# A hybrid trunk layer on one core: w_out begins with P1 and P2, gates run eight tiles ahead, and the last part keeps its written order

## The chip, the cores and the metric

The kernel runs on one core of a Trainium2 chip. The metric is device time in microseconds for one execution of the whole program; three runs of the kernel before gave 2539.71, 2540.99 and 2543.15 us, so the median is 2540.99 us.

## The reference, cut to what matters

One layer for 512 tokens of width 2048, in float32. Two branches read the same normalised input `h`; the change lies in the second half of branch B and in everything behind it.

```python
proj = h @ w_in                                   # 16 kinds of columns, gates among them
...
y_a = o_a @ w_br_a                                # branch A
u = silu(layernorm(conv(glu))) * silu(z_b)
y_b = u @ w_br_b                                  # branch B
gate_a, gate_b = split(sigmoid(gate_logits + b_gate))
mixed = (gate_a * y_a + gate_b * y_b) @ w_out
x = x + rmsnorm(mixed, g_post)
e = p @ w_ple_proj
x = x + rmsnorm(sigmoid(x @ w_ple_gate) * e, g_ple)
```

## The kernel before, in words

**Matrix products.** Every float32 operand is split into a high part (ACT casts it) and a low part (DVE subtracts the cast from the value), and a product is three matmuls: high by high, high by low, low by high. A weight block of 128x1024 floats (512 KB) is loaded by the SP queue into a buffer `raw` (three of them) and split by ACT and DVE into a pair of pieces. Up to branch B the pieces are called `w` (L125, L126), and a tile of 128 output channels by 512 tokens is 48 matmuls of 128x512 (`gemm_cm`, L178, L180 and L182). PSUM gives these tiles two banks (`gps`, L160).

**Branch B.** For each of 16 tiles there is a gate tile (columns of `w_in`, evacuated by ACT with a sigmoid, L700, into a buffer `gt`) and a tile of `w_br_b`, evacuated by DVE: product with the gate (L824), then sum onto branch A's tile (L826). The sum is the tile of `mixed`. The gate tiles run two ahead of the `w_br_b` tiles.

**w_out.** This product of 2048 by 2048 by 512 is done by a scheme of Strassen and Winograd's kind with seven products: in each half `jp` of the output columns there are P1, Q5, P6, P7, P3, P2 and Q4. The left operands come from quarters of `mixed` and their sums (A11, A12, A22, S1 to S4), formed by `split_a`, `split_b` and `split_c`. The right operands are blocks of `w_out` (B11, B12, B22, B21) or sums of them: a tile `t` (B11 plus B12, L972, to which a DMA of POOL that accumulates adds B22 and later B21), and the sum of B12 and B22 for P7 (`sum_t3`, L981). A product is four pieces, and a piece is 12 matmuls, split by `split_piece` (ACT L1016, DVE L1017) three or four pieces ahead. Of the loads after the first eight, every fourth goes to a buffer `rw`, of which there is one. The first half goes (P1, Q5), (P6, P7, P3), (P2, Q4); the second goes (P1, Q5), (P6, P3), (P2), (P7), (Q4). The products in one bracket take turns, piece by piece.

**What becomes of them.** ACT copies the results of P1 and Q5 out of PSUM (`snap`, L1062). DVE adds and subtracts the others (L1066, L1070). `out_fin` then squares a finished tile on ACT with a running sum (L1085) and multiplies it by the broadcast row of `g_post` (`grow`, loaded by the ACT queue, L930) in place on DVE (L1086). When a token group is complete, its RMS factor is formed (L936, L937, POOL L939), `post` adds the residual (L1113; `xr` is x loaded again), and TensorE transposes the result (`x1t`, L1119). The product with `w_ple_gate` follows (L1196 to L1198), the last quarter of which keeps its weights (`hold`), so that the tail of the last token group is short (`ple_last`, L1234 to L1238).

**What sets the order.** The code is written as one sequence of instructions. A scheduler moves the instructions of each engine against that sequence, going by its own estimate of when each can start; each engine then runs its queue strictly in the order it was given.

Of the kernel before, what the change touches and what calls it, by code (L numbers as in the profile page):

```python
# [15 lines left out]
P = 128  # L16
# [66 lines left out]
def _body(ctx, tc, A, out):  # L83
# [19 lines left out]
    nc.gpsimd.memset(mhalf_c, -0.5)  # L103

# [592 lines left out]
    def evac_gate(dst, i, col):  # L697
# [57 lines left out]
    def layer_norm():  # L755
# [35 lines left out]
        rstd = s2.tile([P, T], F32, tag="s2", name="rstd")  # L791
        nc.scalar.copy(rstd, prs)
        yield
        for i in range(NK):
# [9 lines left out]
            ul = low(LOP if i < 32 - LOP else 0, "ul")  # L804
# [40 lines left out]
    def split_a():  # L845
        for k2 in range(4):
            ah = hpool.tile([P, T], F32R, tag="h", name="ah")
            al = hpool.tile([P, T], F32R, tag="h", name="al")
            s1 = slots.tile([P, T], F32, tag="s", name="sf")
            for n in range(2):  # L850
                kk = 2 * k2 + n
                while not (kk in added and kk + 8 in added):
                    yield
                c = slice(n * 256, n * 256 + 256)
                nc.vector.tensor_tensor(s1[:, c], mixed[kk][:, HI], mixed[kk + 8][:, HI], ALU.subtract)
                nc.scalar.copy(ah[:, c], mixed[kk][:, LO])
                nc.vector.tensor_tensor(al[:, c], mixed[kk][:, LO], ah[:, c].bitcast(F32), ALU.subtract)
                yield
            Sf[k2] = s1
            AW["A11"][k2] = (ah, al)  # L860
            AW["S1"][k2] = sw_split(hpool, "h", s1)
            yield

    def split_b():
        for k2 in range(4):
            s1 = Sf.pop(k2)
            s3_ = s3.tile([P, T], F32, tag="s3", name="sf")
            for n in range(2):
                kk = 2 * k2 + n
                c = slice(n * 256, n * 256 + 256)  # L870
                nc.vector.tensor_tensor(s3_[:, c], mixed[kk][:, LO], mixed[kk][:, HI], ALU.subtract)
                nc.vector.tensor_tensor(s1[:, c], s1[:, c], mixed[kk][:, LO], ALU.subtract)
            AW["S3"][k2] = sw_split(hpool, "h", s3_)
            yield
            AW["S2"][k2] = sw_split(hpool, "h", s1)
            for n in range(2):
                kk = 2 * k2 + n
                c = slice(n * 256, n * 256 + 256)
                nc.vector.tensor_tensor(s1[:, c], mixed[kk + 8][:, LO], s1[:, c], ALU.add)
            AW["S4"][k2] = sw_split(slots, "s", s1)  # L880
            yield

    def split_c():
        for kk in range(8):
            CC[kk] = sw_split(*((slots, "s") if kk < 4 else (s3, "s3")), mixed[kk + 8])
            yield
# [3 lines left out]
    def gate_b_tile(i):  # L890
        gemm_cm(w_in_tile(GATE_TILE0 + 16 + i), hT, evac_gate(gate_b, i, 16 + i))

    gate_b_tile(order[0])
    gate_b_tile(order[1])
# [33 lines left out]
    def bcast_row(src, j, home=S3_):  # L928
        t = unit(home, "grow")
        nc.scalar.dma_start(t, src[:, j * T:(j + 1) * T].broadcast_to([P, T]))  # L930
        return t

    def inv_rms(ss, tag):
        n = ss.shape[1]
        tot = fsm.tile([P, n], F32, name="tot" + tag)
        nc.vector.tensor_reduce(tot, ss, AX, ALU.add)  # L936
        nc.vector.tensor_scalar(tot, tot, 1.0 / D, EPS, ALU.mult, ALU.add)  # L937
        r = fsm.tile([P, n], F32, name="rms" + tag)
        nc.gpsimd.tensor_tensor(r, tot, mhalf_c[:, 0:n], ALU.pow)  # L939
        return r  # L940
# [4 lines left out]
    entries = deque()  # L945
    sources = deque()
# [3 lines left out]

    def load(jp, blk, q):
        loads[0] += 1
        if early[0] or loads[0] % 4:
# [3 lines left out]
        nc.sync.dma_start(raw, WO[jp, blk, q])  # L957
        return raw

    early = [True]  # L960
    loads = [0]

    def acc(t, jp, blk, q):
        nc.gpsimd.dma_start(t, WO[jp, blk, q], accum_op=ALU.add)

    def e_a(jp, q):
        early[0] = jp == 0
        b11 = load(jp, B11, q)
        b12 = load(jp, B12, q)
        early[0] = False  # L970
        t = tb[q] = s3.tile([P, 1024], F32, tag="t", name="t", bufs=4)
        nc.vector.tensor_tensor(t, b11, b12, ALU.add)  # L972
        return [b11, t]

    def e_63(jp, q):
        acc(tb[q], jp, B22, q)
        return [tb[q], load(jp, B22, q)]

    def sum_t3(jp, q, b22):
        b12 = load(jp, B12, q)  # L980
        nc.vector.tensor_tensor(b12, b12, b22, ALU.add)  # L981
        return b12

    def e_b(jp, q):
        acc(tb[q], jp, B22, q)
        b22 = load(jp, B22, q)
        return [tb[q], sum_t3(jp, q, b22), b22]

    def e_p7(jp, q):
        return [sum_t3(jp, q, load(jp, B22, q))]  # L990

    def e_p2(jp, q):
        acc(tb[q], jp, B21, q)
        return [load(jp, B21, q)]

    def e_t(jp, q):
        return [tb[q]]

    def e_c(jp, q):
        return e_p2(jp, q) + [tb[q]]  # L1000

    def split_piece():
# [4 lines left out]
        for m in range(2):  # L1007
            if n < 8:
# [7 lines left out]
        nc.scalar.copy(hi, src)  # L1016
        nc.vector.tensor_tensor(lo, src, hi.bitcast(F32), ALU.subtract)  # L1017
# [42 lines left out]
    def snap(home, ps):  # L1060
        t = unit(home, "snap")
        nc.scalar.copy(t, ps)  # L1062
        return t

    def add(dst, a, b):
        nc.vector.tensor_tensor(dst, a, b, ALU.add)  # L1066
        return dst

    def minus(dst, a, b):
        nc.vector.tensor_tensor(dst, a, b, ALU.subtract)  # L1070
# [10 lines left out]
    def out_fin(jp, gp):  # L1081
        def f(tt, n, c):
            j = 2 * jp + n
            junk = unit(S3_, "fjunk")
            nc.scalar.activation(junk, c, AF.Square, accum_out=ssm[:, tt, j:j + 1])  # L1085
            nc.vector.tensor_tensor(c, c, gp[n], ALU.mult)  # L1086
# [14 lines left out]
    def load_x_again(tts):  # L1101
        xr = {}
        for j in range(4):
            for tt in tts:
                xr[tt, j] = unit(HP_, "xr")
                nc.sync.dma_start(xr[tt, j], rows(A["x"], tt, j))
        return xr

    def post(tts, xr):
        rm = inv_rms(ssm[:, tts[0]:tts[0] + 2, :], f"m{tts[0]}")  # L1110
        for j in range(4):
            for n, tt in enumerate(tts):
                nc.vector.scalar_tensor_tensor(x1[tt][j], x1[tt][j], rm[:, n:n + 1], xr.pop((tt, j)), ALU.mult, ALU.add)  # L1113
            yield
            for k2 in (2 * j, 2 * j + 1):
# [5 lines left out]
                nc.scalar.copy(xh, ps)  # L1121
                xl = unit(HP_, "xl", F32R)
                nc.vector.tensor_tensor(xl, ps, xh.bitcast(F32), ALU.subtract)
# [13 lines left out]
    for e, jp in ((e_a, 0), (e_b, 0), (e_c, 0), (e_a, 1), (e_63, 1), (e_p2, 1), (e_p7, 1), (e_t, 1)):  # L1137
        stage(e, jp)

    gen = split_b()  # L1140
    ps = run(("P1", "Q5"), stepper(gen))
    drain(gen)
    s1 = [snap(S3_, x) for x in ps["P1"]]
    s5 = [snap(S3_, x) for x in ps["Q5"]]
    gp = [bcast_row(A["g_post"], j) for j in (0, 1)]
    fin = out_fin(0, gp)
    gen = split_c()
    ps = run(("P6", "P7", "P3"), stepper(gen))
    drain(gen)
    u2 = [add(unit(S3_, "u2"), ps["P6"][t], s1[t]) for t in range(2)]  # L1150
# [5 lines left out]
    ps = run(("P2", "Q4"))  # L1156
    for t in range(2):
# [185 lines left out]
```

## Time and profile before

| | |
|---|---|
| runs | 2539.71, 2540.99, 2543.15 us |
| the profiled execution | 2539.74 us, of it the span 2537.1 us |
| mean granted TensorE clock | 0.997 |
| TensorE busy | 2495.0 us, 98% of the span, 12202 matmuls and transposes |
| VectorE busy | 1652.4 us, 65% |
| ScalarE busy | 1056.8 us, 42% |
| moved by DMA | 279.45 MB, 110 GB/s on average |

Times in a row of the trace are microseconds from the start of the span. "start, duration, engine, line, operation, out<-in" is the form of a row of the timeline; a bracket at its end says how long the engine had been idle and what ended the wait. Matmuls overlap, so the duration of one (0.39 us) is longer than the step from one start to the next; the steps count.

### The profile page before, as it was taken

To read this page: it belongs to the slowest core of one execution; us is meant where nothing else is said; L and a number is where in the kernel's file an instruction comes from. 1 tells how busy PE (TensorE), PEld (TensorE's weight loads), DVE (VectorE), ACT (ScalarE), POOL (GpSimd) and SP (SyncE) were. 2 spreads that over 40 slices of the span, in tenths; PEclk is the share of its full clock that TensorE was granted. 3 is DMA by queue.
4 is the path that set the end of the run, shared out by engine and by line. 5 is a ranking of instruction groups with operands and counts; after the bars stand their busy time and mean duration, and the time that the engine had idled before them with its cause. 6 is when DMAs were issued, how large, how long until landed. Compare 5 with 4: busy or idle time off the path is not lost.

```text
span 2537.1 us, 32634 instructions
## 1 busy us (share of the span) xinstructions
PE 2495.0 (98%) x12202; PEld 2035.7 (80%) x12202; DVE 1652.4 (65%) x3092; ACT 1056.8 (42%) x2083; POOL 140.6 (6%) x151
## 2 busy tenths in 40 slices
PE   8999999999999999999999999999999999999998
PEld 7878787777878777888888888887888888787887
DVE  6765767666676765977786868947433334777644
ACT  6655455455555455322222222225422222544532
POOL 0100000000000000000000000002000000000000
PEclk9999999999999999999999999999999999999999
DMA  6322222222222222333333332442322332677552
GB/s 257 122 87 71 84 72 83 79 75 88 71 84 71 84 67 75 104 105 102 105 97 107 104 107 98 135 135 92 100 99 93 100 99 92 184 214 224 191 174 75
DMA packets 85406, 279.45 MB, mean 110 GB/s; under 512 B 9472, under 2 KB 9728, under 8 KB 85248
## 3 DMA queue, kind: packets, MB, share of 16 engines
q1 hardware_dynamic: 81792, 266.89, 31.5%
q0 software_dynamic: 2304, 8.39, 1.8%
q10 hardware_dynamic: 1152, 2.10, 0.3%
q8 instruction: 95, 1.56, 0.3%
q14 instruction: 63, 0.52, 0.1%
HBM read 262.66 MB, written 14.68 MB: 109 GB/s over the span
## 4 chain that ended last, share of the span: by engine, by line
PE 85%; DVE 9%; ACT 2%; issue 2%; DMA 1%; POOL 0%; SPq 0%; DVEq 0%; POOLq 0%; ACTq 0%
PE g L182 23%; PE g L180 23%; PE g L178 23%; DVE prod L591 2%; PE f L1197 2%; PE f L1198 2%; PE f L1196 2%; DVE w L126 2%; PE psS L469 1%; PE f L1041 1%; PE f L1042 1%; PE f L1040 1%; DVE VT L592 1%; DVE cv L406 1%; PE psB L464 1%
## 5 line engine op out<-in xcount | busy, mean ns | idle before, releaser
L182 PE MATMUL g<-hh,w 128*128 128x512 f32 x2320 | 919.4, 396 | 13.1 <-DVE w L126 13.1
L180 PE MATMUL g<-hl,w 128*128 128x512 f32 x2320 | 915.2, 394 | 0.0
L178 PE MATMUL g<-hh,w 128*128 128x512 f32 x2320 | 914.6, 394 | 0.0
L126 DVE TENSOR_TENSOR w<-raw,w 128x512 fp32r<-128x512 f32 x780 | 549.2, 707 | 483.9 <-ACT w L125 482.8
L125 ACT CAST w<-raw 128x512 fp32r<-128x512 f32 x780 | 478.4, 619 | 893.3 <-PE g L182 789.3
L182 PEld LDWEIGHTS g<-hh,w 128*128 128x128 f32 x2320 | 436.6, 188 | 106.6 <-DVE w L126 21.2
L180 PEld LDWEIGHTS g<-hl,w 128*128 128x128 f32 x2320 | 436.6, 188 | 87.3 <-issue 1.6
L178 PEld LDWEIGHTS g<-hh,w 128*128 128x128 f32 x2320 | 436.8, 188 | 82.9 <-issue 0.2
L673 DVE SCALAR_TENSOR_TENSOR uc<-sg,vec,uc 128x483 f32<-128x483 f32 (+15 forms) x480 | 351.3, 734 | 14.2 <-ACT uc L670 4.3
L406 DVE SCALAR_TENSOR_TENSOR cv<-g,vec,cv 128x511 f32<-128x511 f32 x144 | 107.0, 743 | 32.9 <-ACT cv L404 32.3
L178 PE MATMUL g<-oh,w 128*128 128x512 f32 x256 | 99.6, 389 | 0.0
L180 PE MATMUL g<-ol,w 128*128 128x512 f32 x256 | 99.6, 389 | 0.0
L182 PE MATMUL g<-oh,w 128*128 128x512 f32 x256 | 99.6, 389 | 0.0
L178 PE MATMUL g<-uh,w 128*128 128x512 f32 x256 | 99.6, 389 | 0.0
L180 PE MATMUL g<-ul,w 128*128 128x512 f32 x256 | 99.6, 389 | 0.0
L182 PE MATMUL g<-uh,w 128*128 128x512 f32 x256 | 99.6, 389 | 0.0
L591 DVE TENSOR_TENSOR prod<-UT,VT 128x2 f32<-128x2 f32 (+30 forms) x248 | 87.6, 353 | 7.2
L1041 PE MATMUL f<-wsp,oph 128*128 128x512 f32 x192 | 76.7, 400 | 4.2 <-DVE wsp L1017 4.2
L1197 PE MATMUL f<-w,xh 128*128 128x512 f32 x192 | 75.6, 394 | 2.0 <-DVE w L126 2.0
L1040 PE MATMUL f<-wsp,oph 128*128 128x512 f32 x192 | 75.0, 398 | 1.8 <-ACT wsp L1016 1.8
L1196 PE MATMUL f<-w,xh 128*128 128x512 f32 x192 | 75.8, 396 | 0.0
L1042 PE MATMUL f<-wsp,opl 128*128 128x512 f32 x192 | 75.8, 395 | 0.0
(298 smaller groups left out, 2682.4 us busy)
## 6 DMA issues: line engine op xcount, KB each, us to landing
raw<-in_w_in SPq DMA_DIRECT2D x290, 512.0 KB, 3.3
raw<-in_w_ple_gate SPq DMA_DIRECT2D x40, 512.0 KB, 4.1
raw<-in_w_out SPq DMA_DIRECT2D x35, 512.0 KB, 4.8
raw<-in_w_br_a SPq DMA_DIRECT2D x32, 512.0 KB, 3.3
raw<-in_w_br_b SPq DMA_DIRECT2D x32, 512.0 KB, 3.2
t<-in_w_out POOLq DMA_DIRECT2D x16, 512.0 KB, 7.0
rw<-in_w_out SPq DMA_DIRECT2D x9, 512.0 KB, 4.7
x<-in_x SPq DMA_DIRECT2D x8, 512.0 KB, 9.1
```

What stands on the lines that cost most here:

```text
L125: nc.scalar.copy(hi, rq)
L126: nc.vector.tensor_tensor(lo, rq, hi.bitcast(F32), ALU.subtract)
L178: mm(ps, wh, rh, start=(k == 0), stop=False)
L180: mm(ps, wh, rl, start=False, stop=False)
L182: mm(ps, wl, rh, start=False, stop=(k == NK - 1))
L406: nc.vector.scalar_tensor_tensor(y[:, s:], ps[:, 0:T - s], vv(w0 + 3 - s), y[:, s:], ALU.mult, ALU.add)
L591: nc.vector.tensor_tensor(pv_, um, vm, ALU.mult)
L673: nc.vector.scalar_tensor_tensor(y[:, s:], u[:, 0:T - s], vv(w0 + TAPS - 1 - s), y[:, s:], ALU.mult, ALU.add)
L1041: mm(ps, lh, wl[:, c], start=False, stop=False)
L1042: mm(ps, ll, wh[:, c], start=False, stop=kk == 7)
L1196: mm(ps[tt], lh, wh, start=k == 0, stop=False)
L1197: mm(ps[tt], lh, wl, start=False, stop=False)
```

## The change

In branch B the gate tiles run eight ahead of the `w_br_b` tiles (`AHEAD`). The first two gates go where they went; the others take buffers of the pool `s2`, which `ul` (ten of the low halves of the LayerNorm's output) shares; the small tile `rstd` leaves that pool. `split_mixed` forms the left operands of three quarters while the last eight `w_br_b` tiles run; the fourth quarter, and S3, are formed in the first stage of w_out (`opening`).

The first half of w_out goes (P1, P2), (Q5), (P6, P7, P3), (Q4). P1 and P2 use blocks as loaded. c11, the result of P1 plus P2, is finished before Q5. A sum of two blocks is written where the first of its pieces is needed, and not where its blocks are loaded; the loads of up to two further entries are written ahead of it (`started`). `rw` takes every fourth load from the beginning.

`pin` asks the scheduler to keep the instructions of an engine that are marked so in the written order among each other. It marks the transfers, casts, sums and evacuations of w_out, of the residual, of `w_ple_gate`'s held part and of the end. `xr` takes slots of another pool, and the first reload of x is written behind P6 and P3 of the second half, not ahead of them.

```diff
-            gt = slots.tile([P, T], F32, tag="s", name="gt")
+            gt = (pool or slots).tile([P, T], F32, tag="s2" if pool else "s", name="gt")
...
-        rstd = s2.tile([P, T], F32, tag="s2", name="rstd")
+        rstd = low(0, "rstd", F32)
...
-            ul = low(LOP if i < 32 - LOP else 0, "ul")
+            ul = low(LOP if i < 33 - LOP else 0, "ul")
...
+    AHEAD = 8
...
+    for n in range(2, AHEAD):
+        gate_b_tile(order[n], s2)
     for n, i in enumerate(order):
-        if n + 2 < NK:
-            gate_b_tile(order[n + 2])
-        elif n == NK - 2:
-            jobs.append(lambda: spawn(split_a(), 6, "mix"))
         gemm_cm(A["w_br_b"][i], uT, evac_yb(i))
+        if n + AHEAD < NK:
+            gate_b_tile(order[n + AHEAD], s2)
+        elif n + AHEAD == NK:
+            jobs.append(lambda: spawn(split_mixed(), 12, "mix"))
...
-        if early[0] or loads[0] % 4:
+        if loads[0] % 4:
...
-        nc.sync.dma_start(raw, WO[jp, blk, q])
+        ins = nc.sync.dma_start(raw, WO[jp, blk, q])
+        if loads[0] > 6:
+            pin(ins)
...
     def e_p7(jp, q):
-        return [sum_t3(jp, q, load(jp, B22, q))]
+        b22 = load(jp, B22, q)
+        b12 = load(jp, B12, q)
+        return lambda: [sum_t3(b12, b22)]
...
-        while len(pieces) < ahead and (sources or entries):
-            while len(sources) < 2 and entries:
-                sources.extend(entries.popleft()())
+        while len(pieces) < ahead and (sources or entries or started):
+            while len(sources) < 2 and (entries or started):
+                while entries and len(started) < 2:
+                    started.append(entries.popleft()())
+                sources.extend(started.popleft()())
             split_piece()
...
     gen = split_b()
     ps = run(("P1", "Q5"), stepper(gen))
...
+    gen = opening()
+    ps = run(("P1", "P2"), stepper(gen, 2))
+    drain(gen)
+    s1 = [snap(S3_, x) for x in ps["P1"]]
+    c11 = [add(unit(S3_, "c11"), ps["P2"][t], s1[t]) for t in range(2)]
+    gp = [bcast_row(A["g_post"], j) for j in (0, 1)]
+    fin = out_fin(0, gp)
+    for t in range(2):
+        fin(t, 0, c11[t])
+    ps = run(("Q5",))
+    s5 = [snap(S3_, x) for x in ps["Q5"]]
+    ps = run(("P6", "P7", "P3"))
...
     for t in range(2):
         fin(t, 1, add(d[t], ps["P3"][t], d[t]))
         fin(2 + t, 1, minus(s5[t], s5[t], u3[t]))
-    ps = run(("P2", "Q4"))
-    for t in range(2):
-        fin(t, 0, add(s1[t], ps["P2"][t], s1[t]))
+    ps = run(("Q4",))
...
-            nc.vector.tensor_tensor(c, c, gp[n], ALU.mult)
+            pin(nc.vector.tensor_tensor(c, c, gp[n], ALU.mult))
...
-                nc.scalar.activation(sg[:, c], ps[:, c], AF.Sigmoid)
-                nc.vector.tensor_tensor(e[:, c], sg[:, c], e[:, c], ALU.mult)
+                pin(nc.scalar.activation(sg[:, c], ps[:, c], AF.Sigmoid))
+                pin(nc.vector.tensor_tensor(e[:, c], sg[:, c], e[:, c], ALU.mult))
```

The order on the engines changes at many places. Four of them follow, first TensorE, then three of DVE. On TensorE, where a gate tile follows a tile of `w_br_b` (`uh`, `ul` are branch B's operands, `hh`, `hl` those of the gate's product), there stood before:

```order
L180 MATMUL g<-ul,w 128x512
L182 MATMUL g<-uh,w 128x512
L178 MATMUL g<-hh,w 128x512 [waits Activation_49]
L180 MATMUL g<-hl,w 128x512
L182 MATMUL g<-hh,w 128x512 [waits DVE_49]
```

Now, from the eleventh of the gate's tiles on, there stands (the lines have moved by two):

```order
L182 MATMUL g<-ul,w 128x512
L184 MATMUL g<-uh,w 128x512
L180 MATMUL g<-hh,w 128x512 [waits DVE_49,Activation_49]
L182 MATMUL g<-hl,w 128x512
L184 MATMUL g<-hh,w 128x512
```

The first matmul of the gate tile has a wait for DVE that it did not have; it stands at six gate tiles and at one tile of `w_br_b` behind the last gate, seven places in all. It is for the evacuation (L826 now) of the tile that has just ended, whose bank the new tile takes.

On DVE, behind the pieces of P1 and P2, there stands now a part that has no like before, since c11 was finished at the end of the first half (`c_` is c11, `t` the sums for Q5, the waits DMAHW are for transfers, the one of `c_17722` by `grow` for the row of g_post):

```order
L987 TENSOR_TENSOR t<-raw 128x1024 [waits DMAHW1_49,DMAHW0_49]
L1041 TENSOR_TENSOR wsp<-t,wsp 128x1024 [waits PE_49,Activation_49]
L1094 TENSOR_TENSOR c_17722<-f,snap 128x512 [waits PE_49,Activation_49]
L1094 TENSOR_TENSOR c_17724<-f,snap 128x512 [waits PE_49,Activation_49]
L1114 TENSOR_TENSOR c_17722<-c_17722,grow 128x512 [waits DMAHW5_49,Activation_49]
L1114 TENSOR_TENSOR c_17724<-c_17724,grow 128x512 [waits Activation_49]
L987 TENSOR_TENSOR t<-raw,rw 128x1024 [waits DMAHW3_49,DMAHW2_49]
L1041 TENSOR_TENSOR wsp<-t,wsp 128x1024 [waits Activation_49]
```

The last two rows are the sum for Q5's fourth piece and the low half of its third; they have come to stand behind the products with `grow`.

On DVE, at the end of P6, P7 and P3 of the first half (`d` and `snap` are results being finished), there stood before:

```order
L1066 TENSOR_TENSOR d<-f,d 128x512 [waits PE_49]
L1086 TENSOR_TENSOR d<-d,grow 128x512 [waits DMAHW2_49,Activation_49]
L1086 TENSOR_TENSOR snap<-snap,grow 128x512 [waits Activation_49]
L1086 TENSOR_TENSOR d<-d,grow 128x512 [waits Activation_49]
L1070 TENSOR_TENSOR snap<-snap,u_17946 128x512
L1017 TENSOR_TENSOR wsp<-t,wsp 128x1024 [waits DMASW5_49]
L1017 TENSOR_TENSOR wsp<-raw,wsp 128x1024 [waits DMAHW1_49,PE_49,Activation_49]
L1086 TENSOR_TENSOR snap<-snap,grow 128x512 [waits Activation_49]
L1017 TENSOR_TENSOR wsp<-t,wsp 128x1024 [waits DMASW6_49,PE_49]
```

And now:

```order
L1114 TENSOR_TENSOR d<-d,grow 128x512 [waits DMAHW7_49,Activation_49]
L1098 TENSOR_TENSOR snap<-snap 128x512
L1114 TENSOR_TENSOR snap<-snap,grow 128x512 [waits Activation_49]
L1094 TENSOR_TENSOR d<-f,d 128x512 [waits PE_49]
L1114 TENSOR_TENSOR d<-d,grow 128x512 [waits Activation_49]
L1098 TENSOR_TENSOR snap<-snap 128x512
L1114 TENSOR_TENSOR snap<-snap,grow 128x512 [waits Activation_49]
L987 TENSOR_TENSOR t<-raw 128x1024 [waits DMAHW7_49,DMAHW6_49]
L1041 TENSOR_TENSOR wsp<-t,wsp 128x1024 [waits DMASW7_49,Activation_49]
```

The low halves (`wsp`) that stood among the products with `grow` now stand behind all four, and the last row is that of Q4's fourth piece.

On DVE, where P7 of the second half is prepared, there stood before (L981 is a sum of two blocks, `wsp` a low half):

```order
L1066 TENSOR_TENSOR d<-f,d 128x512 [waits DVE_49,PE_49]
L1017 TENSOR_TENSOR wsp<-rw,wsp 128x1024 [waits DMAHW3_49]
L1086 TENSOR_TENSOR d<-d,grow 128x512 [waits Activation_49]
L1017 TENSOR_TENSOR wsp<-raw,wsp 128x1024 [waits PE_49]
L981 TENSOR_TENSOR rw<-rw,raw 128x1024 [waits DMAHW6_49,DMAHW0_49,DVE_49]
L1066 TENSOR_TENSOR snap<-f,snap 128x512 [waits PE_49]
L981 TENSOR_TENSOR raw<-raw 128x1024 [waits DMAHW7_49,DMAHW1_49,DVE_49]
L1017 TENSOR_TENSOR wsp<-rw,wsp 128x1024 [waits Activation_49]
```

And now:

```order
L1114 TENSOR_TENSOR d<-d,grow 128x512 [waits Activation_49]
L1001 TENSOR_TENSOR raw<-raw 128x1024 [waits DMAHW1_49,DMAHW0_49]
L1041 TENSOR_TENSOR wsp<-rw,wsp 128x1024 [waits DMAHW7_49,Activation_49]
L1001 TENSOR_TENSOR rw<-rw,raw 128x1024 [waits DMAHW3_49,DMAHW2_49,DVE_49]
L1041 TENSOR_TENSOR wsp<-raw,wsp 128x1024 [waits PE_49,Activation_49]
L1001 TENSOR_TENSOR raw<-raw 128x1024 [waits DMAHW5_49,DMAHW4_49,DVE_49]
L1041 TENSOR_TENSOR wsp<-rw,wsp 128x1024 [waits PE_49,Activation_49]
L1001 TENSOR_TENSOR rw<-rw,raw 128x1024 [waits DMAHW6_49,DMAHW0_49,DVE_49]
L1041 TENSOR_TENSOR wsp<-raw,wsp 128x1024 [waits PE_49,Activation_49]
```

The sum for a piece of P7 (`rw<-rw,raw` is that of the second piece) now stands ahead of the low half of the piece before it, where it stood behind.

More of the change, by code (lines that the diff above doesn't have):

```diff
@@ L843, in sw_split @@
         return hi, lo
-    def split_a():
-        for k2 in range(4):
[L847 to L881, printed above, removed]
@@ L886, in split_c, with split_mixed, split_s3, gate_b_tile @@
+    def split_mixed():
+        for k2 in range(3):
+            yield from combine(k2)
+    def split_s3():
+        for k2 in range(4):
+            AW["S3"][k2] = sw_split(s3, "s3", Sf.pop(k2))
             yield
     order = [k + 8 * n for k in range(8) for n in range(2)]
[L890 to L894, printed above, removed]
+    AHEAD = 8
+    def gate_b_tile(i, pool):
+        gemm_cm(w_in_tile(GATE_TILE0 + 16 + i), hT, evac_gate(gate_b, i, 16 + i, pool))
@@ L945, in _body @@
     entries = deque()
+    started = deque()
     sources = deque()
@@ L1135, in drain, with opening @@
             pass
[L1137 removed]
+    for e, jp in ((e_p1p2, 0), (e_q5, 0), (e_b, 0), (e_q4, 0), (sum_t1, 1), (e_63, 1), (e_p2, 1), (e_p7, 1), (e_t, 1)):
         stage(e, jp)
[L1140 to L1141 removed]
+    def opening():
+        yield from combine(3)
+        yield from split_s3()
+    gen = opening()
+    ps = run(("P1", "P2"), stepper(gen, 2))
     drain(gen)
     s1 = [snap(S3_, x) for x in ps["P1"]]
[L1144 removed]
+    c11 = [add(unit(S3_, "c11"), ps["P2"][t], s1[t]) for t in range(2)]
     gp = [bcast_row(A["g_post"], j) for j in (0, 1)]
     fin = out_fin(0, gp)
[L1147 to L1150, printed above, removed]
+    for t in range(2):
[3 more added lines that the diff above has]
+    ps = run(("P6", "P7", "P3"))
+    u2 = [add(s1[t], ps["P6"][t], s1[t]) for t in range(2)]
     d = [minus(unit(S3_, "d"), s5[t], u2[t]) for t in range(2)]
```

145 lines of the change are left out of this document (94 added, 51 removed).

## The prediction

> **What bounds the kernel now.** I read the page's busy times and chain first, then TensorE's windows by stage, then the timeline of the places where it waits.
>
> ```profile
> PE 2495.0 (98%) x12202; PEld 2035.7 (80%) x12202; DVE 1652.4 (65%) x3092; ACT 1056.8 (42%) x2083; POOL 140.6 (6%) x151
> PE 85%; DVE 9%; ACT 2%; issue 2%; DMA 1%; POOL 0%; SPq 0%; DVEq 0%; POOLq 0%; ACTq 0%
> ```
>
> TensorE bounds. The change takes no matmul away and adds none, so all that it can do is to remove or add waits of TensorE and to change the tail. Where the waits are, the windows show: branch B's last part, w_out's opening, its middle, P7 and Q4 of its second half, the entry of `w_ple_gate`, the rest.
>
> ```profile
> core 0: us, PE busy (x) PEld busy (x) DVE busy (x) ACT busy (x) POOL busy (x), PEclk, DMA share, GB/s
> 1840.00:2175.70 335.70, 335.70 (x1483) 278.06 (x1482) 112.81 (x176) 88.41 (x148) 0.00 (x0) 1.00 0.29 96
> 2175.70:2220.00 44.30, 39.60 (x165) 29.84 (x164) 41.44 (x59) 28.00 (x39) 5.41 (x6) 1.00 0.86 227
> 2220.00:2316.00 96.00, 96.00 (x420) 78.58 (x419) 68.78 (x76) 42.27 (x59) 8.68 (x10) 1.00 0.79 227
> 2316.00:2345.70 29.70, 26.75 (x125) 21.34 (x125) 27.12 (x38) 16.31 (x29) 0.73 (x1) 0.94 0.60 201
> 2345.70:2376.00 30.30, 28.34 (x134) 22.77 (x133) 25.62 (x43) 15.59 (x28) 0.70 (x1) 0.94 0.66 218
> ```
>
> Branch B shows the step of TensorE without any wait: 335.70 us over 1483 matmuls is 0.226 us. A tile of 48 is 10.9 us and a piece of 12 is 2.72 us. The opening should take 165 x 0.226 = 37.4 us and takes 44.3, so 6.9 us are lost there. P7 loses what these rows show:
>
> ```profile
> 2317.86 0.40 PE L1040 MATMUL f<-wsp,oph 128*128 128x512 f32 x1
> 2320.40 0.50 PE L1041 MATMUL f<-wsp,oph 128*128 128x512 f32 x1 [2.13 <-DVE wsp L1017]
> ...
> 2321.91 0.63 PE L1041 MATMUL f<-wsp,oph 128*128 128x512 f32 x1
> 2322.34 0.63 PE L1042 MATMUL f<-wsp,opl 128*128 128x512 f32 x1
> ...
> 2327.13 0.40 PE L1042 MATMUL f<-wsp,opl 128*128 128x512 f32 x1
> 2328.35 0.44 PE L1119 MATMUL x1t<-cst,snap 128*128 128x128 f32 x2 [0.82 <-DVE snap L1113]
> ```
>
> The second matmul of P7's second piece waits for its low half: 2.54 - 0.23 = 2.3 us. Then eight matmuls step by 0.43 us, at half pace: 8 x 0.20 = 1.6 us. The transposes lose 1.22 - 0.23 = 1.0. That is 4.9 us in P7, and with the 6.9 of the opening most of what could be won.
>
> [...]
>
> **Branch B.** Running gates ahead needs buffers. Seven gates cannot be evacuated until a `w_br_b` tile has been added to `mixed`, so each holds one of the two banks, and the next tile must take the bank of the tile just ended. TensorE has one such wait already, at the first matmul of w_out:
>
> ```profile
> 2175.80 0.39 PE L182 MATMUL g<-uh,w 128*128 128x512 f32 x1
> 2177.07 0.47 PE L1040 MATMUL f<-wsp,ah 128*128 128x512 f32 x1 [0.88 <-DVE gt L824]
> 2176.23 0.69 DVE L824 TENSOR_TENSOR gt<-g,gt 128x512 f32<-128x512 f32 x1 [4.16 <-PE g L182]
> ```
>
> DVE starts 0.43 us behind the start of the last matmul, takes 0.69, and TensorE's step is 1.27 instead of 0.23: 1.04 us. Nothing hides it. Seven places are 7 x 1.04 = **7.3 us**; the window of branch B shows none of it now. If the waits hid, it would be 0; if a low half stood ahead of the evacuation on DVE, one instruction of 0.69 more, 12.1. The idle time of 0.88 is under the 2.13 that brought half pace. Forming operands meanwhile costs nothing: DVE is busy 112.81 of 335.70 us.
>
> **Opening.** P1 and P2 need no sum, which takes the small waits out, but the bank wait of 1.04 stays, and Q5 now stands alone: four pieces, 10.9 us, from eight loads. Loads and rows land late:
>
> ```profile
> t<-in_w_out POOLq DMA_DIRECT2D x16, 512.0 KB, 7.0
> rw<-in_w_out SPq DMA_DIRECT2D x9, 512.0 KB, 4.7
> grow<-in_g_post ACTq DMA_DIRECT2D x4, 256.0 KB, 6.4
> ```
>
> Counting from branch B's last matmul, P1 and P2 end at 1.3 + 8 x 2.72 = 23.0. Q5's second sum waits for a load in `rw`, which is issued near 18.3, when P2's fourth piece has been split, and lands 4 to 4.7 later. ACT must cast that sum before it copies P1 and issues `grow`, and so gets there at about 25.2. `grow` lands some 6 us later (6.4 at the median), near 31.2. DVE is held there, and behind it stand two products (0.60 each), the sum for the fourth piece (1.14) and the low half of the third (1.2): 34.5, where 29.7 is due. That is 4.8 lost, 1.6 of half pace, 0.8 at Q5's first low half behind the second sum, and 1.04: 8.2 against 6.9, **+1.3 us** (from -5 if `grow` lands in time to +4).
>
> **Into Q4.** The last row of P6, P7 and P3's results is finished on DVE and ACT in turn. These rows give the steps:
>
> ```profile
> 2306.65 0.68 DVE L1066 TENSOR_TENSOR d<-f,d 128x512 f32<-128x512 f32 x1
> 2307.37 0.63 ACT L1085 ACTIVATE fjunk<-d 128x512 f32<-128x512 f32 x1 [1.90 <-DVE d L1066]
> 2307.85 1.22 DVE L981 TENSOR_TENSOR raw<-raw 128x1024 f32<-128x1024 f32 x1
> 2308.98 0.69 DVE L1086 TENSOR_TENSOR d<-d,grow 128x512 f32<-128x512 f32 x1
> ```
>
> An addition and its square take 0.72 + 0.63, then the product 0.60: 2.0 us for each of four results, in strict turn now, because DVE may no longer do other work while it waits for ACT. Six additions before them take 3.6. From 1 to 2 us ahead of Q4's start the chain ends 10 us behind it, then come a sum (1.1) and the low half of Q4's fourth piece (1.2), near 12, due at 8.5. Lost: 3.3 to 5.0, and half pace on top at the most; I take **+3.3 us**, before there was nothing.
>
> **P7 of the second half.** Let P2 begin at 0 (2304.2 now). The loads are tied: P7's second piece goes into `rw` when P2's fourth piece has been split, its fourth when its second has been split.
>
> ```profile
> 2310.19 1.22 DVE L1017 TENSOR_TENSOR wsp<-rw,wsp 128x1024 fp32r<-128x1024 f32 x1
> 2311.43 0.33 SPq L957 DMA_DIRECT2D rw<-in_w_out  x1
> 2311.92 1.22 DVE L1017 TENSOR_TENSOR wsp<-raw,wsp 128x1024 fp32r<-128x1024 f32 x1
> 2315.25 1.23 DVE L981 TENSOR_TENSOR rw<-rw,raw 128x1024 f32<-128x1024 f32 x1 [2.11 <-issue]
> ...
> 2320.37 0.33 SPq L957 DMA_DIRECT2D rw<-in_w_out  x1
> 2325.14 1.23 DVE L981 TENSOR_TENSOR rw<-rw,raw 128x1024 f32<-128x1024 f32 x1 [0.72 <-DMA rw<-in_w_out]
> ```
>
> Before, the low half of P7's first piece was made at 2311.92, in the gap before the load landed (3.8 us after its issue; 4.8 the second time). Now it stands behind the sum. The finishing chain ends at 6.0, a sum at 7.2, the split of `rw` at 8.3; the load lands at 12.2 to 13.2, the sum ends 1.1 later, the low half of the first piece 1.2 later: 14.5 to 15.5, due 11.1. The sum for the third piece needs a load issued at 13.4 to 14.4: low half of the second at 19.5 to 21.5, due 17.2. The sum for the fourth needs `rw` again: low half of the third at 25.7 to 28.7, due 22.2. Two results finished in turn (4.0) and 1.2: the fourth at 30.9 to 33.9, due 28.4. Lost: 3.4 + 2.3 + 3.5 + 2.5 = 11.7 at the early ends, 14.7 at the late ones. Half pace hides in these waits. The transposes then wait for the factor and the residual, 1.4 more. I take 13.1 against 4.9: **+8.2 us**.
>
> **The rest.** At Q4 and the entry of `w_ple_gate` the chain of additions loses about what it lost: 0, from -4 to +4. The tail:
>
> ```profile
> 2527.93 0.66 ACT L1234 ACTIVATE fsg<-f 128x256 f32<-128x256 f32 x2 [9.16 <-PE f L1275]
> 2528.81 0.42 ACT L1237 ACTIVATE fjunk<-e 128x256 f32<-128x256 f32 x1 [0.22 <-DVE e L1235]
> ```
>
> Both sigmoids ran ahead of the first square; now the second stands behind it, so the tail waits for DVE and a square once more: about **+0.9 us**.
>
> The sum is 7.3 + 1.3 + 3.3 + 8.2 + 0.9 = 21.0. On the profiled execution's 2539.74 us that gives 2560.7; it lies 1.25 under the median of the runs, so the median comes to **2562 us**.
>
> **The rivals.** *Faster.* The early operands and the written order remove the 6.9 of the opening but for 1.04, the 4.9 of P7 and about 4 at the gate's entry, 14.8 in all, and only 7.3 and 0.9 are paid: -6.6, 2534 us. It decides if the loads land before DVE reaches the sums; for it speaks that P1 and P2 need no sum, against it that the `rw` load of P7 cannot be issued before about 8 and is needed by 8 to 9. Chance 0.12. *No change*: the opening gains 5 of its 6.9, P7 loses half of what I say, and branch B pays 7.3 less what the earlier operands return, within 5 us of 2541. Chance 0.08. *Banks alone*: the loads land early enough that w_out comes out as before, 7.3 + 0.9: 2549. Chance 0.16. *The forecast*, 2554 to 2570: 0.56. *More half pace*: each of the four waits of P7 and that before Q4 costs 1.6 more, and late ends: 2573. Chance 0.08. That the pins are not kept is ruled out by the order shown.
>
> What can be told from no change is about 0.2%, 5.1 us. Faster by more 0.12, within 0.08, slower 0.80. The range, 2543 to 2570, leaves out the faster case and the worst.
>
> **What would show it.** Seven steps of about 1.27 us between tiles of branch B; none there, and 7.3 falls. A wait of DVE for `grow` in Q5 of 5 us; four waits of TensorE in P7 for low halves, with sums by L1001 directly ahead of them, DVE waiting for transfers. If P7 shows one wait as before, or the opening no wait over 1 us, the forecast is wrong, and the time is near 2549 or less.

## The result and the profile after

The changed kernel takes 2576.02 us at the median of four runs (2575.06 to 2576.97) against 2541.28 of the kernel before: a ratio of 1.0137, 95% interval 1.0125 to 1.015. It is slower by 34.7 us, where the prediction had 21.0, and 6 us above the end of its range.

The page after, TensorE's busy time, the groups of instructions that answer to its waits, and two of the DMA issues:

```profile
PE 2507.0 (97%) x12202; PEld 2040.5 (79%) x12202; DVE 1656.3 (64%) x3092; ACT 1058.8 (41%) x2083; POOL 140.4 (5%) x151
...
L180 PE MATMUL g<-hh,w 128*128 128x512 f32 x2320 | 915.0, 394 | 5.3 <-DVE gt L826 5.3
...
L1069 PE MATMUL f<-wsp,oph 128*128 128x512 f32 x192 | 81.2, 423 | 18.0 <-DVE wsp L1041 18.0
...
t<-in_w_out POOLq DMA_DIRECT2D x16, 512.0 KB, 9.2
rw<-in_w_out SPq DMA_DIRECT2D x12, 512.0 KB, 5.4
```

The group of the low halves in the page before:

```profile
L1041 PE MATMUL f<-wsp,oph 128*128 128x512 f32 x192 | 76.7, 400 | 4.2 <-DVE wsp L1017 4.2
```

The work is the same, 12202 matmuls and transposes. The waits for low halves have grown from 4.2 to 18.0 us, and a wait has come that was not there, for the evacuation at L826. The list of what TensorE waited for in the last part of the changed kernel (total, times, longest):

```profile
PE f L1069 <- DVE wsp L1041: 18.0, 7, 4.3
PE g L180 <- DVE gt L826: 6.1, 7, 0.9
PE f L1068 <- ACT wsp L1041: 6.0, 4, 3.5
PE x1t L1147 <- DVE d L1141: 2.3, 1, 2.3
```

To set stage against stage I take each stage's steps from one matmul to the next and subtract 0.2266 us for a matmul of 128x512, the step where nothing waits, and a quarter of that for a transpose, which is an estimate by the columns (128 against 512); what is left is lost, by a wait or by half pace (matmuls that step by 0.43 us; from 2343.34 to 2349.44, for one, the granted clock is 0.50). In us, with the terms of the prediction beside the measured difference:

| stage | before | after | difference | predicted |
|---|---|---|---|---|
| branch B, gates and `w_br_b` | 0.1 | 7.9 | +7.9 | +7.3 |
| w_out, first half: first 12 pieces, with the wait ahead of them | 7.3 | 16.0 | +8.6 | +1.3 |
| its middle 12 pieces | 0.6 | 1.1 | +0.4 | 0 |
| its last four pieces (Q4 after) | 0.0 | 6.6 | +6.5 | +3.3 |
| second half up to P2's end | 0.6 | 1.3 | +0.7 | 0 |
| P7, with the transposes in it | 5.6 | 15.1 | +9.5 | +8.2 |
| Q4 and the entry of `w_ple_gate` | 7.3 | 10.3 | +3.0 | 0 |
| rest | 0.3 | 0.4 | +0.1 | 0 |
| tail, last matmul to the end of the span | 9.6 | 10.7 | +1.2 | +0.9 |

The differences add up to 37.9; the spans of the two profiled executions are 2575.2 and 2537.1, 38.1 apart. The prediction has 6.9 us for the first 12 pieces before: its window counts 165 matmuls, two of which began ahead of it, so 7.3 is the better figure.

Branch B has its seven steps. One of them:

```profile
1969.33 0.39 PE L184 MATMUL g<-uh,w 128*128 128x512 f32 x1
1970.59 0.47 PE L180 MATMUL g<-hh,w 128*128 128x512 f32 x1 [0.88 <-DVE gt L826]
```

1.26 us instead of 0.23, the same idle time of 0.88 as at the first matmul of w_out.

P7's preparation on DVE, where P2 begins at 2328.4 (after the losses of the table):

```profile
2334.72 1.22 DVE L1001 TENSOR_TENSOR raw<-raw 128x1024 f32<-128x1024 f32 x1
2335.85 1.22 DVE L1041 TENSOR_TENSOR wsp<-rw,wsp 128x1024 fp32r<-128x1024 f32 x1
2340.93 1.23 DVE L1001 TENSOR_TENSOR rw<-rw,raw 128x1024 f32<-128x1024 f32 x1 [3.86 <-DMA rw<-in_w_out]
2342.07 1.22 DVE L1041 TENSOR_TENSOR wsp<-raw,wsp 128x1024 fp32r<-128x1024 f32 x1
2345.57 1.23 DVE L1001 TENSOR_TENSOR raw<-raw 128x1024 f32<-128x1024 f32 x1 [2.28 <-DMA raw<-in_w_out]
2346.71 1.22 DVE L1041 TENSOR_TENSOR wsp<-rw,wsp 128x1024 fp32r<-128x1024 f32 x1
2353.77 1.22 DVE L1001 TENSOR_TENSOR rw<-rw,raw 128x1024 f32<-128x1024 f32 x1 [5.84 <-DMA rw<-in_w_out]
2354.91 1.22 DVE L1041 TENSOR_TENSOR wsp<-raw,wsp 128x1024 fp32r<-128x1024 f32 x1
```

Three times DVE stands idle for a transfer in front of a sum (L1001). TensorE stops for the low half (L1041) behind the first and the third of them:

```profile
2343.34 0.80 PE L1069 MATMUL f<-wsp,oph 128*128 128x512 f32 x1 [3.16 <-DVE wsp L1041]
2356.18 0.75 PE L1069 MATMUL f<-wsp,oph 128*128 128x512 f32 x1 [4.24 <-DVE wsp L1041]
```

The low half behind the second comes while TensorE, at half pace (steps of 0.43 us until 2349.06), is not yet there. The three are done 14.9, 19.6 and 27.8 us behind P2's start, where the prediction had 14.5 to 15.5, 19.5 to 21.5 and 25.7 to 28.7; the fourth (2360.66, 1.22) at 33.5, where it had 30.9 to 33.9.

Q5 of the first half on DVE:

```profile
2208.25 1.23 DVE L987 TENSOR_TENSOR t<-raw,rw 128x1024 f32<-128x1024 f32 x1 [5.22 <-DMA rw<-in_w_out]
2209.40 1.22 DVE L1041 TENSOR_TENSOR wsp<-t,wsp 128x1024 fp32r<-128x1024 f32 x1
...
2215.13 1.29 DVE L1114 TENSOR_TENSOR c<-c,grow 128x512 f32<-128x512 f32 x2 [0.81 <-DMA grow<-in_g_post]
2216.80 1.23 DVE L987 TENSOR_TENSOR t<-raw,rw 128x1024 f32<-128x1024 f32 x1 [0.38 <-DMA rw<-in_w_out]
2217.95 1.22 DVE L1041 TENSOR_TENSOR wsp<-t,wsp 128x1024 fp32r<-128x1024 f32 x1
2225.46 1.23 DVE L1001 TENSOR_TENSOR raw<-raw 128x1024 f32<-128x1024 f32 x1 [6.29 <-DMA raw<-in_w_out]
2226.60 2.35 DVE L1041 TENSOR_TENSOR wsp<-t,wsp 128x1024 fp32r<-128x1024 f32 x2
```

`grow` is used at 2215.13, 31.2 us behind branch B's last matmul, as put down, but DVE waited only 0.8 us for it: the sum ahead had already come late (5.22 us of waiting for `rw`). And a third wait follows which the prediction did not have: the sum for P7's first piece stands ahead of the low half of Q5's fourth piece and waits 6.29 us for its block. The cast of that fourth piece was done at 2219.1, so its low half needed nothing but its turn. In this stretch (2205 to 2236) a load of this queue took 3.6 to 13.0 us to land.

Q4 of the first half begins at 2266.42. Its fourth piece is cast behind the last square:

```profile
2276.52 0.63 ACT L1113 ACTIVATE fjunk<-snap 128x512 f32<-128x512 f32 x1 [1.42 <-DVE snap L1098]
2277.14 1.03 ACT L1041 CAST wsp<-t 128x1024 fp32r<-128x1024 f32 x1
2278.22 1.22 PE L1068 MATMUL f<-wsp,oph 128*128 128x512 f32 x2 [3.45 <-ACT wsp L1041]
```

The tail after:

```profile
2564.90 0.39 ACT L1266 ACTIVATE fsg<-f 128x256 f32<-128x256 f32 x1 [8.29 <-PE f L1307]
2565.77 0.42 ACT L1269 ACTIVATE fjunk<-e 128x256 f32<-128x256 f32 x1 [0.49 <-DVE e L1267]
2566.19 0.36 ACT L1266 ACTIVATE fsg<-f 128x256 f32<-128x256 f32 x1
```

The second sigmoid starts 1.29 us behind the first.

### The profile page after: what moved, and what is told of

Read it like the earlier page. It is cut to its first block, busy times and chain, and to the rows that moved or that the text cites. A ratio compares the mean times of both kernels' runs of the same rounds, so it can differ in the third digit from the quotient of the medians.

```text
span 2575.2 us, 32671 instructions
## 1 busy us (share of the span) xinstructions
PE 2507.0 (97%) x12202; PEld 2040.5 (79%) x12202; DVE 1656.3 (64%) x3092; ACT 1058.8 (41%) x2083; POOL 140.4 (5%) x151
## 4 chain that ended last, share of the span: by engine, by line
PE 84%; DVE 8%; ACT 3%; DMA 2%; issue 2%; POOL 0%; SPq 0%; DVEq 0%; POOLq 0%; ACTq 0%
PE g L184 23%; PE g L182 23%; PE g L180 22%; DVE prod L593 2%; PE f L1229 2%; PE f L1230 2%; PE f L1228 2%; DVE w L128 1%; PE psS L471 1%; DMA raw<-in_w_out 1%; PE f L1069 1%; PE f L1068 1%; PE f L1070 1%; DVE VT L594 1%; DVE cv L408 1%
## 5 line engine op out<-in xcount | busy, mean ns | idle before, releaser
L184 PE MATMUL g<-hh,w 128*128 128x512 f32 x2320 | 919.4, 396 | 13.1 <-DVE w L128 13.1
L1069 PE MATMUL f<-wsp,oph 128*128 128x512 f32 x192 | 81.2, 423 | 18.0 <-DVE wsp L1041 18.0
L1068 PE MATMUL f<-wsp,oph 128*128 128x512 f32 x192 | 77.9, 416 | 6.0 <-ACT wsp L1041 6.0
L1228 PE MATMUL f<-w,xh 128*128 128x512 f32 x192 | 75.2, 392 | 0.0
L1230 PE MATMUL f<-w,xl 128*128 128x512 f32 x192 | 75.0, 391 | 0.0
```

The lines of the kernel that those rows point to most:

```text
L184: mm(ps, wl, rh, start=False, stop=(k == NK - 1))
L1069: mm(ps, lh, wl[:, c], start=False, stop=False)
L1228: mm(ps[tt], lh, wh, start=k == 0, stop=False)
L1230: mm(ps[tt], ll, wh, start=False, stop=k == NK - 1)
```

## The experiments

The theory: what is lost in w_out is lost through the written order on DVE and ACT, and 7.3 us of branch B through the buffer that eight gates lack. The rival: the order of the products and the transfers lose it, whoever waits. All stage losses below are made as in the table.

**Seven gates ahead.**

```diff
-    AHEAD = 8
+    AHEAD = 7
```

> The changed kernel with the gate tiles seven ahead instead of eight; nothing else differs (the operands begin to be formed one tile later). Seven gates fit the seven free buffers, so no gate holds a bank. If the seven waits of branch B are the buffers' doing, they go (7 x 1.04 = 7.3 us) and the time falls from 2576 to about 2569; w_out loses what it lost. If the waits are only the sign of something else (DVE late with the evacuation because it forms operands), five or more of them stay and the time stays within 3 us of 2576.

2568.32 us, 7.7 below; branch B loses 0.1 instead of 7.9, w_out and what follows 49.3 instead of 50.6. The waits are the buffers'.

**Nothing pinned.**

```diff
-    pin = tc.keep_in_program_order
+    pin = lambda ins: ins
```

> The changed kernel with no instruction pinned; the order of products, the early operands and eight gates ahead stay. Theory: the written order of DVE and ACT makes most of w_out's loss. Then P7 of the second half falls from 15 us lost to about 5, the entry of Q4 of the first half from 6.7 to 1 or less, the tail by 0.9, and the opening by a part; the time is about 2555. Rival: the order of the products and the transfers make the loss (Q5 alone needs eight loads in 10.9 us). Then the opening keeps its 16 us and P7 most of its 15, and the time stays above 2568.

2550.60 us, 25.4 below. P7 loses 5.7 instead of 15.1, the end of the first half 0.0 instead of 6.6, Q5's stretch (the last four of the first 12 pieces) 7.8 instead of 14.7. The longest waits that are left:

```profile
PE g L180 <- DVE gt L826: 6.1, 7, 0.9
PE f L1069 <- DVE wsp L1041: 6.0, 3, 2.5
PE f L1229 <- DVE w L128: 1.9, 1, 1.9
```

The low halves are down from 18.0 to 6.0 us and the waits for ACT's casts nearly gone.

**Sums written late.**

```diff
-            while len(sources) < 2 and (entries or started):
+            while len(sources) < 1 and (entries or started):
```

> The changed kernel, pinned, but a sum is written only when no source is left, so that it stands behind the low half of the piece before it and no longer ahead of it. Theory: a sum that waits for its load holds the low half behind it. Then P7 loses 5 to 8 us instead of 15, Q5 of the first half some 5 less than its 15, and the time is about 2560 to 2566. Rival: the loads themselves come too late whatever stands behind them (one buffer rw, transfers at their limit). Then the waits only move from the low half to the cast, and the time stays within 4 us of 2576.

2567.97 us, 8.1 below, between what the two expected. Q5's stretch falls from 14.7 to 10.5, P7 only from 15.1 to 12.3, and the waits move, as the rival said, from the low half to the cast:

```profile
PE f L1068 <- ACT wsp L1041: 14.2, 4, 7.1
...
PE f L1069 <- DVE wsp L1041: 2.6, 5, 0.8
```

So the place of the sums alone does not explain P7.

**Seven gates and nothing pinned.** The first two edits together.

> Both of the first two: gates seven ahead and nothing pinned. If the two costs are independent, it is 7.3 us below the kernel without pins, near 2548 by the theory (so the early operands and the new order of products bring nothing against the kernel before, 2541), and near 2561 or more by the rival.

2543.36 us, ratio to before 1.0011 (1.0001 to 1.0021). It is 7.2 us below the kernel without pins, so the two costs add. What remains of the change, early operands and the new order of products among it, gains nothing.

**Without POOL's accumulating transfers.**

```diff
-        pin(nc.gpsimd.dma_start(t, WO[jp, blk, q], accum_op=ALU.add))
+        pass
```

> The changed kernel without the accumulating transfers of POOL (16 of 512 KB): the tiles t keep B11 plus B12, so P6, Q4 and P3 work on the wrong sums; every other instruction stays. Theory: beside the order, the transfers of w_out's opening are at their limit, since P1, P2 and Q5 need 16 loads, the rows of g_post come in the same stretch, and POOL's transfers add to them; so loads land 5 to 13 us after their issue where 4 to 4.7 were put in. Then without POOL's the opening loses 9 to 12 us instead of 16, and the time falls by 4 to 8 us. Rival: the loads are late only because buffers come free late (the order again). Then the opening stays within 2 us of its 16.

2568.60 us, 7.4 below; Q5's stretch loses 7.6 instead of 14.7, every other stage what it lost within 0.5 us. The opening as a whole loses 8.8, and the rival, with 16, is out. DVE at the same place as above:

```profile
2215.94 1.23 DVE L987 TENSOR_TENSOR t<-raw,rw 128x1024 f32<-128x1024 f32 x1 [0.26 <-DMA rw<-in_w_out]
2217.08 1.22 DVE L1041 TENSOR_TENSOR wsp<-t,wsp 128x1024 fp32r<-128x1024 f32 x1
2219.51 1.23 DVE L1001 TENSOR_TENSOR raw<-raw 128x1024 f32<-128x1024 f32 x1 [1.22 <-DMA raw<-in_w_out]
```

The block lands 6 us earlier, and the wait is 1.22 us instead of 6.29. It was issued only 0.7 us earlier but took 7.7 us instead of 13.0, each the slowest load of its stretch. The mean share of the 16 DMA engines between 2212 and 2226 is 0.68, where it was 1.03. So Q5's third wait, which is gone here (2.74 and 2.17 us for low halves stay, against 2.93, 2.33 and 4.28), comes from a load that takes 13.0 us beside POOL's transfers and 7.7 without them.

**Pins on transfers alone, and on the rest alone.** The one keeps `pin` for the issues of SP, ACT and POOL's transfers, the other for casts, sums, evacuations and the small work of POOL. The issues are given a name of their own at each place, and one of the two names does nothing:

```diff
-            pin(ins)
+            pin_dma(ins)
...
-        pin(nc.gpsimd.dma_start(t, WO[jp, blk, q], accum_op=ALU.add))
+        pin_dma(nc.gpsimd.dma_start(t, WO[jp, blk, q], accum_op=ALU.add))
```

> The changed kernel with the pins on transfers alone (SP, ACT's and POOL's issues); casts, sums and evacuations may be moved again. Theory: the loss of the pins sits on DVE and ACT, where an instruction that waits holds those behind it. Then this kernel is within 4 us of the one without any pin (2550.6). Rival: the written order of the loads (x's reload and the rows among them) is what makes them late. Then it stays above 2562.

> The changed kernel with the pins on casts, sums and evacuations alone; transfers may be moved again. Theory: it stays within 5 us of the changed kernel (2576). Rival: below 2562.

2548.93 us and 2580.18 us. The first is as fast as the kernel without pins, the second no better than the changed kernel, both as the theory had it. The loss is made on DVE and ACT. The written order of loads costs nothing in sum; by stage Q5's stretch loses 10.3 instead of 7.8 with it, and P7 3.1 instead of 5.7.

**The old order of products.** Seven gates ahead, nothing pinned, operands still formed during branch B; the loads follow the products (not shown).

```diff
-    ps = run(("P1", "P2"), stepper(gen, 2))
+    ps = run(("P1", "Q5"), stepper(gen, 2))
...
-    ps = run(("Q5",))
...
-    ps = run(("Q4",))
+    ps = run(("P2", "Q4"))
```

> Gates seven ahead, nothing pinned, the left operands still formed during branch B, but the first half of w_out in its old order: (P1, Q5), (P6, P7, P3), (P2, Q4). Against the kernel with seven gates, no pins and the new order (2543.4) this changes the products' order alone. Theory: P1 with P2 and then Q5 alone costs the opening 3 to 4 us because Q5's eight loads crowd into 10.9 us; then this kernel loses 7 us or less there and takes about 2539 to 2541, and the early operands by themselves are worth 0 to 2 us against the kernel before. Rival: the opening is as slow in the old order, since the operands are not what it waits for; then it stays at 2543 or above.

2541.78 us, 1.0002 (0.9992 to 1.0011), within what cannot be told from 2543.4. The opening loses 10.7 us, against 10.5 with the new order: as slow, as the rival said, though the time lies between the two expectations. Of it 6.8 is one wait, behind a sum of a block in `rw`. That load was issued at 2184.31 and landed 11.7 us later, beside two of POOL's transfers (8.9 and 9.6 us).

**The first eight loads not in `rw`.** In the last kernel, and in the one with the new order of products:

```diff
-        if loads[0] % 4:
+        if loads[0] <= 8 or loads[0] % 4:
```

> The kernel with seven gates ahead, nothing pinned and the old order of products (2541.8), in which the first eight loads of w_out no longer use the one buffer rw, as in the kernel before. Its opening waits 7 us at one place, for the fourth pair of blocks, one of which goes to rw. Theory: that wait is rw's, which is free for its second load only when the first has been split; without it the opening loses 4 us or less and the time is 2535 to 2538, below the kernel before: what the early operands are worth. Rival: the wait is for the transfers at their limit, whatever buffer they go to. Then the opening still loses 9 us or more, and the time stays at 2541 or above.

> The same change of rw to the kernel with seven gates ahead, nothing pinned and the new order of products (2543.4). If rw's early use makes what this opening loses (11 us), it falls by 4 us or more, to 2539 or less; if Q5 alone with its eight loads makes it, it stays within 2 us of 2543.

2539.79 us (0.9997, 0.9988 to 1.0006) and 2544.02 (1.0015, 1.0006 to 1.0024). In both the opening changes by less than 1 us in sum (10.1 and 9.6 lost); the wait at the fourth pair goes and others come. So the opening's loss is not `rw`'s: by the loss the rival holds in the first, though its time is not at 2541, and the second stays within 2 us as its second case had it. The early operands do not bring what they were hoped to bring there.

**The finishing free.** Additions, subtractions, squares and products with `grow` are not pinned, everything else is.

```diff
-        pin(nc.vector.tensor_tensor(dst, a, b, ALU.add))
+        nc.vector.tensor_tensor(dst, a, b, ALU.add)
...
-        pin(nc.vector.tensor_tensor(dst, a, b, ALU.subtract))
+        nc.vector.tensor_tensor(dst, a, b, ALU.subtract)
...
-            pin(nc.scalar.activation(junk, c, AF.Square, accum_out=ssm[:, tt, j:j + 1]))
-            pin(nc.vector.tensor_tensor(c, c, gp[n], ALU.mult))
+            nc.scalar.activation(junk, c, AF.Square, accum_out=ssm[:, tt, j:j + 1])
+            nc.vector.tensor_tensor(c, c, gp[n], ALU.mult)
```

> The changed kernel with the finishing of results free to move (additions, subtractions, squares and products with the row of g_post are not pinned); loads, sums of blocks and splits stay pinned. Theory of the prediction: at the entry of Q4 of the first half TensorE waits because the chain of additions, squares and products stands ahead of Q4's fourth piece; free, its 6.7 us go to 1 or less, and P7 keeps 8 us or more of its 15, because the sums still stand ahead of the splits. The time is 2560 to 2568. Rival: the splits wait for loads there, not for the chain. Then the entry of Q4 keeps 5 us or more.

2565.82 us, 10.2 below. The end of the first half loses 0.0 instead of 6.6: that term was the finishing chain, as predicted. P7 still loses 12.4.

**The old order of products with pins on transfers.** The kernel of 2539.79 us, transfers alone pinned.

> The first kernel of this group with the transfers alone pinned. With the new order of products such pins brought the time from 2550.6 to 2548.9, which is no difference beyond the intervals. If the written order of loads helps, this kernel is 1 to 3 us below the one without pins; otherwise the same within 2 us or slower.

2536.96 us, ratio 0.9984 (0.9975 to 0.9993): the only version here whose interval lies below the kernel before, by less than the 0.2% that the prediction calls a change. It is 2.8 us below the kernel without pins, as the first case had it, though the two intervals overlap; its opening loses 6.8 instead of 10.1 us. From w_out on its profile loses 21.7 us, the kernel before 21.8, so the trace does not say where a gain over that kernel would come from.

**P7 again: late sums and free finishing together.** Two of the edits above; loads, sums and splits stay pinned.

> The changed kernel with the finishing of results free and the sums written behind the low half of the piece before; loads, sums and splits stay pinned. P7 of the second half lost 15.1 us in the changed kernel, 12.3 with late sums alone and 12.4 with free finishing alone, 5.5 with nothing pinned. Theory: either of the two orders is enough to make the load into rw late or to hold a low half, so only both together help: P7 loses 5 to 8 us here, and the time is 2555 to 2560. Rival: neither of them is P7's cause, but the written order of splits and loads among each other. Then P7 still loses 11 us or more.

2551.85 us. P7 loses 5.1, near the 5.7 with nothing pinned, against 12.3 and 12.4 with one of the two. Either order alone is enough to hold the stage, and the rival, the order of splits and loads among each other, is out.

**Sums and splits free, all else pinned.**

```diff
-            pin(nc.vector.tensor_tensor(t, b11, b12, ALU.add))
+            nc.vector.tensor_tensor(t, b11, b12, ALU.add)
...
-        pin(nc.vector.tensor_tensor(b12, b12, b22, ALU.add))
+        nc.vector.tensor_tensor(b12, b12, b22, ALU.add)
...
             if n >= 3:
-                pin(ins)
+                pass
```

> The changed kernel with the sums of blocks and the splits into high and low halves free, and the finishing, residual, x's transposed halves and transfers still pinned. Theory: the splits may then go ahead of the finishing chain and of a sum that waits, so P7 loses 5 to 7 us, the entry of Q4 of the first half 1 or less, and the time is 2550 to 2556. Rival: the finishing chain holds more than the splits; then the entry of Q4 keeps 4 us or P7 10 or more.

2552.32 us: 23.7 of the 25.4 us that all pins cost go with these three lines. The end of the first half loses 0.0, P7 6.0. What costs is that splits are held behind the finishing chain and behind sums. It can be undone from either side: the kernel before this one (2551.85) has its splits pinned and is as fast, with the chain free and each sum behind the low half of the piece before.

**No pins and no accumulating transfers.**

> The changed kernel with nothing pinned and without POOL's accumulating transfers (P6, Q4 and P3 work on the wrong sums). Q5 of the first half lost 14.7 us in the changed kernel, 7.6 without POOL's transfers, 7.8 without pins. If order and transfers are two causes that add, it loses 2 us or less here; if both act through the same wait (loads that are issued late and then land late), it still loses 5 us or more.

2545.66 us. Q5's stretch loses 6.1; with pins alone gone it was 7.8, with the transfers alone gone 7.6. They do not add: either edit takes away the same wait, the third. Two are left, 1.23 us for a low half behind a sum (DVE waits 3.66 us there for `rw`) and 2.67 us for one behind the products with `grow` (2.97 us). These are the two places that the prediction named. Whether Q5 standing alone makes them stays open.

## Why the prediction was half right

**Branch B (+7.3): right.** Measured 7.9, by seven waits of 0.88 us or a little less and steps of about 1.26; with seven gates ahead all of it goes.

**The opening (+1.3): the step that failed.** Measured +8.6: it loses 16.0 us where the sum had 8.2. The bank wait came as put down (1.0, with P1 and P2 1.2). So did the third low half behind `grow`'s products: put at 4.8 and 1.6 of half pace, it cost 4.5. The first low half behind the second sum was put at 0.8 and cost 3.2. By the prediction's own landing times (22.3 to 23.0, then 1.1 and 1.2, where 23.5 is due) it comes to 1.1 to 1.9; the rest is a load that was issued 0.9 us later and took 5.1 us instead of 4 to 4.7. And the sum stopped at Q5's third piece, so the fourth low half stood in it at nothing, without a reason. It stands behind P7's first sum, the very pattern that the prediction priced in P7 and nowhere else, and cost 7.0: 4.28 us of waiting and half pace for the 13 matmuls behind it, until 2233.4 (granted clock 0.50). Why the block for that sum came so late the run without POOL's transfers shows: without them it landed 7.7 us after its issue instead of 13.0. The medians of the kernel before (4.7 for `rw`, 7.0 for `t`) were taken for a stretch in which they no longer held (the page after has 5.4 and 9.2).

**Into Q4 (+3.3): the mechanism right, the size that of the late end and half pace.** The chain was 2.0 us per result as put down (an addition at 2269.43, the product behind its square at 2270.90, the next result's at 2272.98). It ends 11.5 us behind Q4's start, where 10 was put down, and the cast of the fourth piece stands behind its last square as the low half does behind its last product. TensorE waits 3.45 us for that cast and then runs at half pace (granted clock 0.50 from 2278.22 to 2284.58), together 6.6: the 5.0 of the late end and the 1.6 that had been left out of the value taken.

**P7 (+8.2): right in its times, incomplete in its cause.** Measured +9.5; the stage loses 15.1, inside the 13.1 to 16.1 that its two ends and the transposes make, where the early end was taken. The low halves came within the ranges. TensorE stopped long for two of the four only (3.16 and 4.24 us), and half pace (steps of 0.43 us) covered the others but for 0.53 us, as the prediction let it. It named the sum ahead of the low half as what makes the difference. That is one of two: with the sums late, or the finishing free, 12 us stay; with both, 5.1.

**Q4 and the entry of `w_ple_gate` (0, from -4 to +4): +3.0,** inside its bounds. **Tail (+0.9): 1.2.** Together the prediction's sum was 21.0, the measured one 37.9. Of the missing 16.9 the opening accounts for 7.3, Q4 of the first half, Q4 of the second and the entry of `w_ple_gate` for 6.2, P7 for 1.3.

**The rivals.** Faster and no change needed loads that land before DVE reaches the sums; DVE waited 5.2, 6.3, 3.9, 2.3 and 5.8 us for transfers instead. *More half pace* (2573) came nearest in number, but not for its reason: before Q4 of the first half its 1.6 came, in P7 nothing came on top of the forecast's bounds. That w_out comes out as before (2549) is what happens without pins (2550.60).

## What to carry to other kernels

A written order is as good as its worst wait. Here DVE stood idle for a load for 6.29 us in front of a sum, while a low half that TensorE needed stood ready behind it. So pin the transfers and leave the splits free; where the splits are pinned, the finishing must be free and the sums written late. When a pattern has been found that costs 3 us at one place (a sum ahead of the low half of the piece before), look for it at every stage that is written by the same code. Work moved ahead must have buffers for its full distance: with one buffer too few, eight tiles ahead cost seven bank waits of some 0.9 us, and seven ahead none.

## What was not expected of the hardware

Half pace does not go by the length of one idle time alone. In the changed kernel an idle time of 2.93 us was followed by full pace, one of 2.33 us by half pace:

```profile
2210.67 0.50 PE L1069 MATMUL f<-wsp,oph 128*128 128x512 f32 x1 [2.93 <-DVE wsp L1041]
2219.22 0.50 PE L1069 MATMUL f<-wsp,oph 128*128 128x512 f32 x1 [2.33 <-DVE wsp L1041]
```

Behind the first the granted clock is 1.00 (2210.67 to 2216.15), and the matmuls step by 0.23 us. Behind the second the clock is 0.50 (2219.82 to 2223.14), and they step by 0.43 us. Behind a third idle time, again of 2.33 us, ahead of a transpose at 2384.46, the clock is 1.00.

In the profiles of the kernel before and of the changed one, from 100 us on, TensorE stood idle for 1.96 to 4.28 us twelve times, each time coming from full pace. Half pace followed nine times, all but behind the 2.93 us, the 2.33 us ahead of the transpose and 2.04 us at 2377.41. It followed none of the 42 idle times from 0.3 to 1.26 us. What decides between 1.96 and 2.93 us these profiles do not show.
